# Prompt attention: the weights' division by their row sums moved from separate passes into the products that transpose them

## The chip, the cores and the metric

The kernel runs on one core of a Trainium2 chip. The metric is the device time of one execution in microseconds (us), lower is better. Engines are named as in the profile: PE is the TensorE matmul pipe (PEld its weight loads), DVE is VectorE, ACT is ScalarE, POOL is GpSimd, SP issues the DMAs.

## The reference, cut to what matters

One layer of a decoder for 1024 prompt tokens and 64 sample tokens, with a model width of 2048: a normalised and modulated input `h`, one input projection, three mixers side by side (dilated attention with 12 heads of 64, a spatial-gating MLP, an mLSTM), one output projection, a gate and the residual. The change lies in the attention of the prompt:

```
s = q k^T + bias                (per head, masked to the pattern; 1024 x 1024, causal)
p = exp(s - max(s)) / sum(exp(s - max(s)))      (over the keys)
o = p v
y_a = o * silu(z_a)
```

All inputs and outputs are float32. The reference forms three dilated patterns and combines them by their softmax denominators; the kernel does it in one softmax, with the logarithm of how many patterns hold a key added to the bias table.

## The kernel before, in words

Everything is kept with features on the partitions and the 1088 tokens on the free axis. The kernel goes through the input projection column by column (L252 to L254 are its three products: each weight tile and each input is split into a high and a low part of type float32r, and high times high, high times low and low times high are added up), and weaves the mixers' work between the columns. The prompt's attention is left for the last stage, where it is woven into the output projection.

**The last stage.** `project` runs twice over 16 output tiles. The first run takes the ten blocks of 128 features that the other two mixers have made (in pieces of 4, 2 and 4 blocks), the second the six blocks of the attention. For each piece and each of the three stretches of tokens (512, 320 and 256) it issues its products (`products`, L252 to L254) and then calls `tick()` once per block. Every call adds 0.345 to a counter, and each time this passes 1 the attention's generator does one step. So each engine's order of instructions is fixed when the program is written: some nine products of the projection, then one step of the attention, and so on. What is left of the attention after the first run is drained, and the second run follows.

**One step of the attention** (`attention`) may issue the value products of a block pair (`values`), the scores of a block of 128 queries (`scores`), the transposition of one block pair (`turn`), and what is due on ACT and DVE (`due`, sorted by the second number of `at`).

- `scores(e, m)` handles two blocks of queries, r = 0 and r = 1, with `nk = 128 * (2m + r + 1)` keys. Two products (L1445, L1446) put 512 columns of scores into PSUM, one DVE instruction (L1448) adds the bias, writes them to the tile `P` in SBUF and finds the rows' maxima. One step later ACT takes the exponential in place and sums the rows (`expo`, L1457). Two steps later `norm` takes the reciprocal of the sums (L1460, DVE) and multiplies the whole row of weights by it in place: for r = 1 on DVE (L1462), for r = 0 on ACT (L1464). The `P` tile is 256(m + 1) wide, so that for r = 0 its last 128 columns are not used.
- `turn(e, m, P, po, j)` makes up to four transposes (L1487) of 128 queries by 128 keys into the PSUM tile `pt`, three where the block pair lies on the diagonal. ACT copies `pt` to the high part `pH` (L1488), DVE subtracts to make the low part `pL` (L1489).
- `values` multiplies the value rows with `pH` (L1496) and `pL` (L1498) and adds up in PSUM; after the last pair the result is gated (L1502 to L1507) and stored.

`prep` fetches the next head's keys, queries, values and bias table; there POOL makes the low parts (L1406, L1411, L1417). POOL also makes the low parts of the weights (L99).

**Rows from other stages.** Four more lines serve the prediction for their durations. In the mLSTM, `first` issues a plain product of 128 by 128 (L938) and two transposes of the same size (L939, L940), one after the other, and L1003 is a product whose stationary operand has 32 columns. In the gating MLP L1148 is a plain product of 128 by 128, in fours. All of them have operands of type float32, without the high and low parts of the projection.

Of the kernel before, what the change touches and what calls it, by code (L numbers as in the profile page):

```python
# [11 lines left out]
FT = mybir.dt.float32  # L12
FR = mybir.dt.float32r
I32 = mybir.dt.int32
AF = mybir.ActivationFunctionType
OP = mybir.AluOpType
# [6 lines left out]
NSM = NB * NT  # L23
# [88 lines left out]
def body(tc, I, O):  # L112
    nc = tc.nc
    V, S, T, G, SP = nc.vector, nc.scalar, nc.tensor, nc.gpsimd, nc.sync
# [3 lines left out]
    def pool(name, st=None, **kw):  # L118
        return (st or stack).enter_context(tc.tile_pool(name=name, **kw))

    cp = pool("consts", bufs=1)
# [5 lines left out]
    bgs = ExitStack()  # L127
# [5 lines left out]
    def et(name="e"):  # L133
        return ev.tile([128, 388], FT, tag="e", name=name, bufs=7)
# [71 lines left out]
    def C(name, a=None, b=None, rows=128, r0=0):  # L206
        o, w = FO[name]
        a = 0 if a is None else a
        b = w if b is None else b
        return cst[r0:r0 + rows, o + a:o + b]  # L210

    ident = C("ident")
# [42 lines left out]

    ND9 = 9
    gate = cp.tile([128, KT, ND9], FT, name="gate")
    knew = cp.tile([128, 2, 2, NSM], FT, name="knew")
    qg8 = cp.tile([128, 1], FT, name="qg8")
    V.tensor_scalar(qg8, C("qg"), 0.125, None, op0=OP.mult)  # L260

# [276 lines left out]
    for k in range(2):  # L538
        for c, (t0, n) in enumerate(CH):
            for j in range(NST):  # L540
                ps = mm.tile([128, 512], FT, tag="mm", name="mm")
                wh, wl = w0[j // 2]
                o = 256 * (j % 2) + 128 * k
# [206 lines left out]
    st0.close()  # L750


    sel = pool("qk", bgs, bufs=1).tile([96, 3, 128], FR, name="sel")
    t = et("sel")
    SP.dma_start(t[:96, :128], I["sel"][:96])
    V.memset(sel.bitcast(FT), 0.0)
    for c in range(3):
        r = slice(32 * c, 32 * c + 32)
# [457 lines left out]
    def sample(qd):  # L1216
# [18 lines left out]
        for hf in range(2):  # L1235
# [49 lines left out]

            os_ = bank("os")
            pts = [turn(0)]
            yield
            pts.append(turn(1))
            yield  # L1290
            for i in range(5):
                v = kv_get()
                for x in range(2):
                    for b in range(4):
                        T.matmul(os_[32 * b:32 * b + 32, :256], pts[i][:, 128 * x + 32 * b:128 * x + 32 * b + 32],  # L1295
                                 v[:, b, 256 * x:256 * x + 256], start=(i == 0 and x == 0), stop=False,
                                 skip_group_check=True)
                if i < 4:
                    pts.append(turn(i + 2))
                yield  # L1300
# [82 lines left out]
    tp = pool("att", st4, bufs=1)  # L1383
# [43 lines left out]
    def at(d, order, f):  # L1427
        due.append((clk[0] + d, order, f))


    def scores(e, m):

        P = []
        for r in range(2):
            qb = 2 * m + r
            nk = 128 * (qb + 1)
            a = slice(128 * qb, 128 * qb + 128)
            s = tp.tile([128, 256 * (m + 1)], FT, tag=f"P{m}", name="P", bufs=2)
            mx = tp.tile([128, 6], FT, tag="mx", name="mx", bufs=6)
            np_ = 0  # L1440
            for k0 in range(0, nk, 512):
                w = min(512, nk - k0)
                wide = max(w, 256)
                ps = aps.tile([128, 512], FT, tag="a", name="s", bufs=5)
                T.matmul(ps[:, :wide], e["qs"][:, a], e["kd"][:, k0:k0 + wide], start=True, stop=False)  # L1445
                T.matmul(ps[:, :wide], e["qs"][:, a], e["kl"][:, k0:k0 + wide], start=False, stop=True)  # L1446
                x = k0 + 896 - 128 * qb
                V.tensor_tensor_reduce(s[:, k0:k0 + w], ps[:, :w], e["bt"][:, x:x + w], 1.0,  # L1448
                                       mx[:, np_ - 1:np_] if np_ else -3.0e38, op0=OP.add, op1=OP.max,
                                       accum_out=mx[:, np_:np_ + 1])  # L1450
                np_ += 1
                if k0 + 512 < nk:
                    yield
            V.tensor_scalar(mx[:, 2:3], mx[:, np_ - 1:np_], -1.0, None, op0=OP.mult)

            def expo(s=s, mx=mx, nk=nk):
                S.activation(s[:, :nk], s[:, :nk], AF.Exp, bias=mx[:, 2:3], accum_out=mx[:, 3:4])  # L1457

            def norm(s=s, mx=mx, nk=nk, r=r):
                V.reciprocal(mx[:, 4:5], mx[:, 3:4])  # L1460
                if r:
                    V.tensor_scalar(s[:, :nk], s[:, :nk], mx[:, 4:5], None, op0=OP.mult)  # L1462
                else:
                    S.activation(s[:, :nk], s[:, :nk], AF.Copy, scale=mx[:, 4:5])  # L1464

            at(1, 0, expo)
            at(2, 1, norm)
            P.append(s)
            if r or m:
                yield  # L1470
        return P

    def turn(e, m, P, po, j):

        pt = aps.tile([128, 512], FT, tag="a", name="pt", bufs=5)
        pH = tp.tile([128, 512], FR, tag="pH", name="pH", bufs=3)
        pL = tp.tile([128, 512], FR, tag="pL", name="pL", bufs=3)
        f = 128 if j == m else 0
        if f:
            V.memset(pH[:, 0:128].bitcast(FT), 0.0)  # L1480
            V.memset(pL[:, 0:128].bitcast(FT), 0.0)
        for b in range(2):
            for r in range(2):
                k = 128 * (2 * j + b)
                o = 256 * (1 - b) + 128 * r
                if o >= f:
                    T.transpose(pt[:, o:o + 128], P[r][:, k:k + 128], ident)  # L1487
        S.copy(pH[:, f:], pt[:, f:])  # L1488
        at(0, 3, lambda: V.tensor_tensor(pL[:, f:], pt[:, f:], pH[:, f:].bitcast(FT), op=OP.subtract))  # L1489
        return pH, pL  # L1490
# [21 lines left out]
    def all_scores(e):  # L1512
        for hd in range(HA):
            pg = prep(hd + 1) if hd + 1 < HA else loads(KB[:3])
            nxt = None
            for m in range(4):
                g = scores(e, m)
                while True:
                    try:
                        next(g)  # L1520
                    except StopIteration as x:
                        P = x.value
                        break
                    yield
                    if pg is not None and m and clk[0] % 2:
                        try:
                            next(pg)
                        except StopIteration as x:
                            nxt, pg = x.value, None
                po = []  # L1530
                for j in range(m + 1):
                    tq.append((clk[0] + 2, (e, m, P, po, j)))
            while pg is not None:
                try:
                    next(pg)
                except StopIteration as x:
                    nxt, pg = x.value, None
            e = nxt
# [250 lines left out]
```

## Time and profile before

| what | before |
|---|---|
| median of 3 runs | 2487.4 us (2485.78 to 2488.67) |
| profiled execution, its time | 2489.15 us |
| its span | 2487.2 us |
| PE busy | 2435.5 us, 98% of the span |
| DVE busy | 939.0 us, 38% |
| ACT busy | 746.2 us, 30% |
| POOL busy | 646.5 us, 26% |

The span runs from the first to the last instruction of the profiled execution; the other 1.95 us of its time lie around it. In the rows of groups, the two numbers after the first bar are the busy time in us and the mean of one instruction in ns, and behind the second bar stand the idle time of the engine ahead of them in us and what ended it. A matmul's own duration counts from its start to its modelled end, and the next one starts before that end; how many ns a matmul takes of a dense stream is read from the chain of work, whose pieces do not overlap.

### The profile page before, as it was taken

The page shows a single profiled execution, that of the slowest core. Times are in us where ns is not written, and L with a number is a line of the kernel's source. Part 1 is how long each engine was busy: PE and PEld are TensorE (multiplying, and loading weights), DVE is VectorE, ACT ScalarE, POOL GpSimd, SP SyncE. Part 2 cuts the span into 40 slices and gives each one's busy share as a digit, 9 for nine tenths or more (in the row PEclk, how much of TensorE's full clock was granted, in tenths as well). Part 3 has the DMA queues.
Part 4 walks back from the last instruction along what each step waited for, and adds up shares of the span by engine and source line. Part 5 has one row for each costly group of instructions (what it writes and reads, how often), then busy time and mean ns, then how long its engine had stood idle before and what let it go on. Part 6 is the DMA issues. An engine that isn't in the chain of part 4 may idle for free.

```text
span 2487.2 us, 39837 instructions
## 1 busy us (share of the span) xinstructions
PE 2435.5 (98%) x15879; PEld 2228.4 (90%) x15879; DVE 939.0 (38%) x2489; ACT 746.2 (30%) x1638; POOL 646.5 (26%) x502
## 2 busy tenths in 40 slices
PE   5999999999999999999999999999999999999999
PEld 2678799999999999999999999898889899888898
DVE  4673100323232322313342002433212688887322
ACT  3222211323223232323321112222113566666210
POOL 2541122231312222322222222111212333332321
PEclk8999999999999999999999999999999999999999
DMA  8864621111211111121313415746565655554454
GB/s 280 287 231 146 223 68 39 57 65 53 63 55 57 62 60 53 48 74 49 118 58 101 153 48 213 255 164 236 207 222 193 198 158 155 150 151 134 159 170 143
DMA packets 157081, 332.95 MB, mean 134 GB/s; under 512 B 21770, under 2 KB 76834, under 8 KB 149216
## 3 DMA queue, kind: packets, MB, share of 16 engines
q1 hardware_dynamic: 156896, 330.41, 40.8%
q8 instruction: 125, 2.05, 0.4%
q14 instruction: 60, 0.49, 0.1%
HBM read 284.26 MB, written 54.55 MB: 136 GB/s over the span
## 4 chain that ended last, share of the span: by engine, by line
PE 91%; DVE 3%; DMA 3%; issue 1%; ACT 1%; SPq 1%; POOL 0%; DVEq 0%; ACTq 0%; POOLq 0%
PE mm L252 26%; PE mm L254 25%; PE mm L253 25%; PE ad L342 2%; PE pt L1487 2%; PE os L1295 1%; PE sq L1245 1%; PE o L1498 1%; PE s L1446 1%; PE o L1496 1%; PE s L1445 1%; DMA x<-in_xT 1%; DMA ad<-in_adaw 1%; PE b L938 0%; PE b L970 0%
## 5 line engine op out<-in xcount | busy, mean ns | idle before, releaser
L252 PE MATMUL mm<-hH,wh 128*128 128x384 f32 (+1 forms) x3168 | 1063.2, 336 | 10.0 <-ACT hH L425 8.4
L253 PE MATMUL mm<-hL,wh 128*128 128x384 f32 (+1 forms) x3168 | 1034.4, 327 | 2.6 <-DVE hL L431 2.6
L254 PE MATMUL mm<-hH,wl 128*128 128x384 f32 (+1 forms) x3168 | 1035.8, 327 | 0.0
L99 POOL TENSOR_TENSOR wl<-wraw,wh 128x512 fp32r<-128x512 f32 x344 | 445.7, 1303 | 1570.2 <-ACT wh L98 1466.8
L252 PEld LDWEIGHTS mm<-hH,wh 128*128 128x128 f32 x3168 | 595.5, 188 | 75.3 <-issue 40.0
L253 PEld LDWEIGHTS mm<-hL,wh 128*128 128x128 f32 x3168 | 595.9, 188 | 4.7 <-DVE hL L431 3.6
L254 PEld LDWEIGHTS mm<-hH,wl 128*128 128x128 f32 x3168 | 594.9, 188 | 0.0
L98 ACT CAST wh<-wraw 128x512 fp32r<-128x512 f32 x344 | 200.9, 596 | 379.9 <-PE mm L253 269.6
L252 PE MATMUL mm<-yH,wh 128*128 128x512 f32 (+2 forms) x768 | 262.3, 341 | 2.8 <-DVE xo L1583 2.8
L254 PE MATMUL mm<-yH,wl 128*128 128x512 f32 (+2 forms) x768 | 252.3, 329 | 1.1 <-POOL wl L99 1.1
L253 PE MATMUL mm<-yL,wh 128*128 128x512 f32 (+2 forms) x768 | 252.4, 329 | 0.0
L254 PEld LDWEIGHTS mm<-yH,wl 128*128 128x128 f32 x768 | 145.3, 189 | 12.5 <-POOL wl L99 1.5
L252 PEld LDWEIGHTS mm<-yH,wh 128*128 128x128 f32 x768 | 145.4, 189 | 12.2 <-issue 3.0
L253 PEld LDWEIGHTS mm<-yL,wh 128*128 128x128 f32 x768 | 145.6, 190 | 8.9
L894 DVE SCALAR_TENSOR_TENSOR u<-R,cw,u 128x384 f32<-128x384 f32 (+1 forms) x108 | 62.0, 574 | 213.4 <-ACT u L892 210.8
L1583 DVE SCALAR_TENSOR_TENSOR xo<-mm,gate,xo 128x512 f32<-128x512 f32 (+2 forms) x96 | 54.3, 568 | 116.1 <-PE mm L254 107.8
L1488 ACT CAST pH<-pt 128x512 fp32r<-128x512 f32 (+1 forms) x120 | 65.2, 543 | 81.1 <-PE pt L1487 80.4
L1489 DVE TENSOR_TENSOR pL<-pt,pH 128x512 fp32r<-128x512 f32 (+1 forms) x120 | 74.1, 618 | 15.6 <-ACT pH L1488 15.5
L1457 ACT ACTIVATE P<-P,mx 128x128 f32<-128x128 f32 (+3 forms) x96 | 74.5, 777 | 4.2 <-issue 2.9
L1487 PE MATMUL pt<-cst,P 128*128 128x128 f32 x432 | 68.9, 274 | 6.3 <-DVE P L1462 5.9
L1487 PEld LDWEIGHTS pt<-cst,P 128*128 128x128 f32 x432 | 52.7, 140 | 19.3 <-DVE P L1462 9.2
L1448 DVE CUSTOM_DVE_ANT_0 P<-s,btab 128x512 f32<-128x512 f32 (+2 forms) x96 | 56.1, 584 | 34.2 <-PE s L1446 33.9
(324 smaller groups left out, 2409.7 us busy)
## 6 DMA issues: line engine op xcount, KB each, us to landing
wraw<-in_win SPq DMA_DIRECT2D x264, 256.0 KB
ad<-in_adaw SPq DMA_DIRECT2D x96, 512.0 KB
kv<-in_ck SPq DMA_DIRECT2D x30, 1024.0 KB
kv<-in_cv SPq DMA_DIRECT2D x30, 1024.0 KB
wraw<-in_wout SPq DMA_DIRECT2D x48, 256.0 KB
x<-in_xT SPq DMA_DIRECT2D x16, 544.0 KB
yraw<-yD SPq DMA_DIRECT2D x16, 544.0 KB
xo<-in_xT SPq DMA_DIRECT2D x16, 544.0 KB
```

The lines of the kernel that those rows point to most:

```text
L98: self.nc.scalar.copy(wh[:, :n], raw[:, :n])
L99: self.nc.gpsimd.tensor_tensor(wl[:, :n], raw[:, :n], wh[:, :n].bitcast(FT), op=OP.subtract)
L252: T.matmul(ps[:, :n], wh[:, a], rh[:, t0:t0 + n], start=first and i == 0, stop=False)
L253: T.matmul(ps[:, :n], wh[:, a], rl[:, t0:t0 + n], start=False, stop=False)
L254: T.matmul(ps[:, :n], wl[:, a], rh[:, t0:t0 + n], start=False, stop=last and i == len(rows) - 1)
L894: V.scalar_tensor_tensor(u[:, :npr], R[:, j:j + npr], cw[:, m, j:j + 1], u[:, :npr], op0=OP.mult, op1=OP.add)
L1448: V.tensor_tensor_reduce(s[:, k0:k0 + w], ps[:, :w], e["bt"][:, x:x + w], 1.0, mx[:, np_ - 1:np_] if np_ else -3.0e38, op0=OP.add, op1=OP.max,
L1457: S.activation(s[:, :nk], s[:, :nk], AF.Exp, bias=mx[:, 2:3], accum_out=mx[:, 3:4])
L1487: T.transpose(pt[:, o:o + 128], P[r][:, k:k + 128], ident)
L1488: S.copy(pH[:, f:], pt[:, f:])
L1489: at(0, 3, lambda: V.tensor_tensor(pL[:, f:], pt[:, f:], pH[:, f:].bitcast(FT), op=OP.subtract))
L1583: V.scalar_tensor_tensor(x[:, t0:t0 + npr], ps[:, :npr], gate[:, dm, 0:1], x[:, t0:t0 + npr], op0=OP.mult, op1=OP.add)
```

## The change

The weights stay as ACT's exponential left them. For each block of queries `norm` now makes a diagonal matrix of 128 by 128, the identity times the reciprocal sums (one DVE instruction, L1463 of the changed kernel). For r = 0 it goes to the free columns of `P`, for r = 1 to a tile of its own, `dg`, with three buffers. The passes of L1462 and L1464 are gone. In `turn`, where a transpose stood (the data as the stationary operand, the identity as the moving one), a product stands now: the data as the stationary operand, the diagonal matrix as the moving one. So out of `pt` come the transposed weights, already divided. The tile `knew`, used in an earlier stage alone, moves to a pool that is closed before the last stage.

```
-    knew = cp.tile([128, 2, 2, NSM], FT, name="knew")
...
-    sel = pool("qk", bgs, bufs=1).tile([96, 3, 128], FR, name="sel")
+    qkp = pool("qk", bgs, bufs=1)
+    sel = qkp.tile([96, 3, 128], FR, name="sel")
+    knew = qkp.tile([128, 2, 2, NSM], FT, name="knew")
...
             mx = tp.tile([128, 6], FT, tag="mx", name="mx", bufs=6)
+            dg = tp.tile([128, 128], FT, tag="dg", name="dg", bufs=3) if r else s[:, nk:nk + 128]
...
-            def norm(s=s, mx=mx, nk=nk, r=r):
+            def norm(mx=mx, dg=dg):
                 V.reciprocal(mx[:, 4:5], mx[:, 3:4])
-                if r:
-                    V.tensor_scalar(s[:, :nk], s[:, :nk], mx[:, 4:5], None, op0=OP.mult)
-                else:
-                    S.activation(s[:, :nk], s[:, :nk], AF.Copy, scale=mx[:, 4:5])
+                V.tensor_scalar(dg, ident, mx[:, 4:5], None, op0=OP.mult)
...
-            P.append(s)
+            P.append((s, dg))
...
                 if o >= f:
-                    T.transpose(pt[:, o:o + 128], P[r][:, k:k + 128], ident)
+                    T.matmul(pt[:, o:o + 128], P[r][0][:, k:k + 128], P[r][1], start=True, stop=True)
```

On PE, in the middle of the second head's scores, the order before has the four transposes of a pair (`pt<-cst,P`) between the next scores and the projection:

```order
L1446 MATMUL s<-kl,qs 128x512
L1487 MATMUL pt<-cst,P 128x128 x4
L252 MATMUL mm<-yH,wh 128x256
L253 MATMUL mm<-yL,wh 128x256
L254 MATMUL mm<-yH,wl 128x256
```

In the changed kernel the same place reads as follows. `pt<-P` is a product whose diagonal matrix lies in `P` itself (r = 0), `pt<-dg,P` one with the tile `dg` (r = 1); the scores' lines have moved by two.

```order
L1448 MATMUL s<-kl,qs 128x512
L1487 MATMUL pt<-P 128x128
L1487 MATMUL pt<-dg,P 128x128
L1487 MATMUL pt<-P 128x128
L1487 MATMUL pt<-dg,P 128x128
L252 MATMUL mm<-yH,wh 128x256
```

Four instructions stand in the place of four, and nothing else of PE's order has moved; over the program 432 transposes became 432 products.

On DVE, at the place where the third pair of query blocks of a head is normalised (m = 2, r = 1), before:

```order
L1481 MEMSET pL 128x128
L1460 RECIPROCAL mx<-mx 128x1
L1462 TENSOR_SCALAR P<-P,mx 128x768
L1505 TENSOR_TENSOR t<-o,t 64x256
L1507 SCALAR_TENSOR_TENSOR t<-t,zt 64x256
```

And with the change:

```order
L1481 MEMSET pL 128x128
L1462 RECIPROCAL mx<-mx 128x1
L1463 TENSOR_SCALAR dg<-cst,mx 128x128
L1505 TENSOR_TENSOR t<-o,t 64x256
L1507 SCALAR_TENSOR_TENSOR t<-t,zt 64x256
```

The pass over 768 columns has become one over 128 in the same place; where r = 0, one over 128 is new on DVE right behind the reciprocal, and ACT's pass is gone without anything in its place. The orders of POOL and of SP are the same in both kernels, and so is every engine's order ahead of the attention's first `norm`.

## The prediction

> **What bounds the kernel now.** I read the busy times of the page first, then the chain that ended last, then the stretch of the last stage in which the attention runs, 1945 to 2320 us after the span's start.
>
> ```profile
> span 2487.2 us, 39837 instructions
> PE 2435.5 (98%) x15879; PEld 2228.4 (90%) x15879; DVE 939.0 (38%) x2489; ACT 746.2 (30%) x1638; POOL 646.5 (26%) x502
> ```
>
> ```profile
> PE 91%; DVE 3%; DMA 3%; issue 1%; ACT 1%; SPq 1%; POOL 0%; DVEq 0%; ACTq 0%; POOLq 0%
> ```
>
> ```profile
> core 0: us, PE busy (x) PEld busy (x) DVE busy (x) ACT busy (x) POOL busy (x), PEclk, DMA share, GB/s
> 1945.00:2320.00 375.00, 365.61 (x2428) 332.35 (x2428) 296.95 (x908) 236.36 (x487) 125.54 (x80) 1.00 0.53 150
> ```
>
> PE is busy for 98% of the whole span, 91% of the chain is PE, and the stretch that the change touches is no different: 365.6 of its 375.0 us, at the full granted clock (1.00). DVE (297.0 us, 79%) and ACT (236.4 us, 63%) have room there. So a change in this stretch is worth what it does to PE's own stream, plus what it does to the 9.4 us in which PE stands. The waits of PE in that stretch say whom it stands for:
>
> ```profile
> engine line waited for: us in total, times, longest us
> PE pt L1487 <- DVE P L1462: 5.9, 6, 1.5
> PE o L1498 <- DVE pL L1489: 1.8, 4, 1.1
> PE o L1496 <- ACT pH L1488: 1.2, 1, 1.2
> PE pt L1487 <- DVE mx L1448: 0.3, 1, 0.3
> ```
>
> They make 9.2 us. The largest is the pass that the change removes from DVE, and the transposes of L1487 are what waits for it; but it is 5.9 us in 6 events, of 120 groups of transposes.
>
> **What it removes: two sets of passes.** The groups of that stretch, L1462 with its four widths apart:
>
> ```profile
> L1462 DVE TENSOR_SCALAR P<-P,mx 128x256 f32<-128x256 f32 x12 | 4.2, 354 | 0.4
> L1462 DVE TENSOR_SCALAR P<-P,mx 128x512 f32<-128x512 f32 x12 | 11.2, 931 | 0.4
> L1462 DVE TENSOR_SCALAR P<-P,mx 128x768 f32<-128x768 f32 x12 | 12.7, 1060 | 0.5
> L1462 DVE TENSOR_SCALAR P<-P,mx 128x1024 f32<-128x1024 f32 x12 | 10.7, 894 | 0.4
> ...
> L1464 ACT ACTIVATE P<-P,mx 128x128 f32<-128x128 f32 (+3 forms) x48 | 34.5, 720 | 12.1 <-DVE mx L1460 12.0
> ...
> L1480 DVE MEMSET pH<- 128x128 f32 x48 | 7.9, 165 | 0.0
> ```
>
> DVE loses 4.2 + 11.2 + 12.7 + 10.7 = 38.8 us, ACT 34.5 us. Neither engine is the bound, so none of these 73 us comes off the time by itself. They count only through PE's 9.2 us of waits.
>
> **What it adds on DVE: 96 diagonal matrices of 128x128.** The trace has no such instruction. From below it is bounded by the store of the same size without an input, 165 ns (L1480), from above by the same operation on twice the columns, 354 ns (L1462, 128x256). I take 290 ns, nearer to the latter since it is the same operation with half the columns: 96 x 0.29 = 28 us. For r = 0 this is new work on DVE, for r = 1 a shorter pass. DVE's sum falls by about 11 us, ACT's by 34.5 us, and this hides beside PE, as the passes did. If that cover were gone, 28 us is the most that it could cost.
>
> **What it adds on PE: 432 products for 432 transposes.** This is the term that decides. What a transpose takes of PE's stream is shown by two pieces of the chain, a group of four and one of three where PE waits for nothing:
>
> ```profile
> 1970.48 0.44 PE pt L1487 x4
> ```
>
> ```profile
> 1973.67 0.33 PE pt L1487 x3
> ```
>
> That is 110 ns each, and by 432 it is 47.5 us of the stretch. A plain product of the same size and type does not stand at this place before, but elsewhere in the same program there are some. First, how many records one makes: L938 is a plain product and L939 a transpose, issued by the same loop side by side, so that both stand equally often in the program.
>
> ```profile
> L938 PE MATMUL b<-qT,kT 128*128 128x128 f32 x96 | 18.5, 274 | 0.0
> L939 PE MATMUL b<-cst,kT 128*128 128x128 f32 x48 | 13.1, 273 | 0.0
> ```
>
> The product leaves 96 records where the transpose leaves 48: on this chip a float32 product is carried out as two matmuls, each with its weight load, and the transpose as one. Then what they take of the stream, again from the chain:
>
> ```profile
> 764.06 0.22 PE b L938 x2
> 764.28 0.11 PE b L939
> ```
>
> ```profile
> 1260.89 0.89 PE mx L1148 x8
> ```
>
> One product (L938, two records) takes 0.22 us, and the transpose right behind it 0.11 us. Four products of L1148 in a row, with the same shapes as the change's four, are eight records and 0.89 us, or 222.5 ns for one. So each exchange costs 222.5 - 110 = 112.5 ns, and 432 of them 432 x 0.1125 = 48.6 us. Nothing hides it: PE's stream is dense in the whole stretch, and the projection's products stand right behind.
>
> On this the Trainium skill, "TensorE: Matmul & The Clock Gate", section Terms, has a rule that speaks against the change even more: it says that the transpose mode is 4 times faster for FP32. By that rule the exchange would cost three transposes' time, and the sum would be 142.6 us in place of 48.6. The rows above show a factor of two at this size, and the measurement decides; the rule is kept as a rival below.
>
> **What becomes of PE's waits.** The transposes wait for exponential, reciprocal and pass; now for exponential, reciprocal and a diagonal matrix. At m = 2 the pass at its shortest takes twice what I put for the matrix, so that some tenths of a us of each of the 6 waits go. But much of such a wait isn't the length of the pass. The stretch around 2101 us, in order of time:
>
> ```profile
> 2101.16 2.40 POOL L1406 TENSOR_TENSOR kl<-kr,kd 128x1024 fp32r<-128x1024 f32 x1 [3.21 <-ACT kd L1405]
> 2101.26 2.58 DVE L1462 TENSOR_SCALAR P<-P,mx 128x512 f32<-128x512 f32 x1
> ```
>
> The pass over 512 columns started 0.10 us behind a POOL instruction of 2.40 us and took 2.58 us, though the pass over 1024 columns takes 0.89 us on the mean. DVE's pass stood until POOL was through. The diagonal matrix is the same operation on the same engine, with both operands in SBUF, and will stand likewise; now for r = 0 as well, where ACT did it without such a wait. The Trainium skill, "SBUF — State Buffer", section Who interferes with whom, names tensor_scalar among the operations that can take a port pair shared with GpSimd, the later one being blocked fully; the two rows agree. So one gain (shorter passes, 34.5 us less on ACT, 11 us less on DVE, also for `pH` and `pL`) stands against one loss (96 exposed instructions instead of 48). The ends: all 9.2 us of waits go, or they double. I take a third gone, -3.1 us, since the load on both engines falls and the stretch grows by an eighth.
>
> Where a wait goes, next is the projection's product behind it, which needs weights that POOL makes two pieces ahead. The wait for the buffers of `dg` (three, each freed by the last product of its pair of query blocks) falls behind no work: a buffer comes round again with the third pair after it, and is written seven steps or more behind the pair's last scores, while the pair's products are issued two to five steps behind them. `knew` is written in an earlier stage in the same place of DVE's order, and its move costs nothing.
>
> **The sum.** 48.6 - 3.1 = +45.5 us. Against the profiled execution (2489.15 us, of which 2487.2 is the span) that is 2534.7 us; this execution lies 1.75 us above the median of the runs, 2487.4 us, and a median is what is measured, so I forecast 2487.4 + 45.5 = 2533 us (rounded).
>
> **Rivals.**
>
> *The diagonal matrices stand behind POOL and PE stands behind them.* The shortest passes of the three wider forms, in the order of time:
>
> ```profile
> 1977.03 0.75 DVE L1462 TENSOR_SCALAR P<-P,mx 128x1024 f32<-128x1024 f32 x1
> ```
>
> ```profile
> 1983.46 0.49 DVE L1462 TENSOR_SCALAR P<-P,mx 128x512 f32<-128x512 f32 x1
> ```
>
> ```profile
> 2026.45 0.62 DVE L1462 TENSOR_SCALAR P<-P,mx 128x768 f32<-128x768 f32 x1
> ```
>
> Twelve of each, with 0.35 us for 256 columns, are 26.5 us; the 48 passes took 38.8 us, so 12.3 us were standing. 96 exposed instructions would stand 24.6 us; if all of it reaches PE beside the old waits, the time is 2487.4 + 48.6 + 24.6 = 2560.6 us. For it: PE did wait for L1462. Against: of 12.3 us that stood, PE felt at most 5.9, and the matrices of r = 0 are made a step ahead of those of r = 1 wherever m is above 0. Chance 0.06.
>
> *Four transposes' time for a product.* 432 x 3 x 0.110 = 142.6, less 3.1: 2626.9 us. The rows of L938 and L1148 speak against it, and nothing in the trace for it. Chance 0.02.
>
> *Not slower: the second matmul of a product costs next to nothing here.* The point from which this decides: with all 9.2 us of waits gone, a product may take 110 + 9200/432 = 131 ns for no loss. One row shows matmuls from float32 operands that follow each other so fast, those of L1003, whose stationary operand has 32 columns:
>
> ```profile
> 771.70 1.01 PE b L1003 x16
> ```
>
> It is 63 ns a record, 126 ns a product; 432 x 0.016 - 9.2 = -2.3, or 2485 us. Against: the change's stationary operand has 128 columns, as L1148's, and all rows of that shape show 0.11 us a record. Chance 0.03.
>
> *The change doesn't do what it says:* the product with a diagonal matrix is carried out as one matmul like a transpose. Then only waits go, 3.1 to 9.2 us, around 2481 us. L938 and L1148 speak against it. Chance 0.02.
>
> **How the numbers follow.** The forecast has 0.87. Its own bounds are the waits' ends, 2487.4 + 48.6 - 9.2 = 2526.8 and 2487.4 + 48.6 + 9.2 = 2545.2, with the runs' spread of about 1.5 us at either end: 2525 to 2547. These leave out 0.13 for the rivals, so the range need not reach to them. A measurement of this kernel can tell about 0.2%, 5 us, from no change. Faster by more than that comes from parts of the last two rivals, 0.03; within it, 0.02; slower, 0.95.
>
> **What would show it.** Right: L1487 with 864 records, groups of eight at 0.89 us in the chain, the stretch of the attention about 45 us longer with PE still at 97% or more, all other stages as before; DVE with 96 instructions of 0.2 to 0.35 us in the place of L1462, some of over 1 us when POOL is at work. Wrong: 432 records, or eight of them well under 0.8 us; PE waits for the diagonal matrices of 20 us and more; or a stage ahead of the attention that has moved.

## The result, and the profile after

| what | before | after |
|---|---|---|
| median of 4 runs | 2486.9 us (2485.78 to 2488.67) | 2529.76 us (2527.79 to 2535.3) |
| ratio to before | | 1.0172, 95% interval 1.0159 to 1.0184 |
| profiled execution, its span | 2487.2 us | 2525.7 us |

The kernel became slower by 42.9 us between the medians; 45.5 were forecast. The busy times of the page after, and the group of products with the tile `dg`, with its counterpart for r = 0:

```profile
span 2525.7 us, 40801 instructions
PE 2482.0 (98%) x16311; PEld 2283.3 (90%) x16311; DVE 957.8 (38%) x2537; ACT 715.5 (28%) x1590; POOL 644.7 (26%) x502
...
L1487 PE MATMUL pt<-dg,P 128*128 128x128 f32 x480 | 85.5, 276 | 2.6 <-DVE dg L1463 2.6
...
L1487 PE MATMUL pt<-P 128*128 128x128 f32 x384 | 73.9, 274 | 0.2 <-DVE mx L1450 0.2
```

PE has 16311 - 15879 = 432 records more, and L1487 has 480 + 384 = 864, where it had 432. In order of time on PE, a group of four of them in the second head (the chain of after covers the last stretch alone, so the stream is read from the starts):

```profile
1969.27 0.38 PE L1487 MATMUL pt<-P 128*128 128x128 f32 x2
1969.49 0.39 PE L1487 MATMUL pt<-dg,P 128*128 128x128 f32 x2
1969.71 0.39 PE L1487 MATMUL pt<-P 128*128 128x128 f32 x2
1969.93 0.39 PE L1487 MATMUL pt<-dg,P 128*128 128x128 f32 x2
```

Each product has two records, and the next one starts 0.22 us later. Where the attention's stretch begins and ends is read from its first score product and its last subtraction, in the rows of the tiles `s` and `pL`. Before:

```profile
L1445 PE MATMUL s<-kd,qs x144: 274/364/398, 1947.7 to 2297.0; 128*128 128x512 f32 x72, 128*128 128x256 f32 x48, 128*128 128x384 f32 x24
```

```profile
L1489 DVE TENSOR_TENSOR pL<-pt,pH x120: 486/674/692, 1954.5 to 2314.8; 128x512 fp32r<-128x512 f32 x72, 128x384 fp32r<-128x384 f32 x48
```

And after:

```profile
L1447 PE MATMUL s<-kd,qs x144: 277/389/415, 1944.0 to 2334.5; 128*128 128x512 f32 x72, 128*128 128x256 f32 x48, 128*128 128x384 f32 x24
```

```profile
L1489 DVE TENSOR_TENSOR pL<-pt,pH x120: 485/675/693, 1951.8 to 2354.1; 128x512 fp32r<-128x512 f32 x72, 128x384 fp32r<-128x384 f32 x48
```

From 1947.7 to 2314.8 are 367.1 us, from 1944.0 to 2354.1 are 410.1 us: +43.0 us, the whole of the change. That the stretch begins 3.7 us earlier in the one profiled execution after is mostly from the first 400 us, where the inputs arrive (PE was busy for 369.65 us there and for 366.97 before); the change has nothing in that stage, and the runs of one kernel differ by as much.

PE's waits in the stretch after, and its busy time:

```profile
engine line waited for: us in total, times, longest us
PE pt L1487 <- DVE dg L1463: 2.6, 5, 1.0
PE o L1498 <- DVE pL L1489: 1.6, 3, 0.9
PE pt L1487 <- DVE mx L1450: 0.2, 1, 0.2
```

```profile
1944.00:2357.00 413.00, 408.46 (x2840) 382.60 (x2839) 314.05 (x954) 203.88 (x435) 119.96 (x77) 1.00 0.48 136
```

The waits fell from 9.2 to 4.4 us. The diagonal matrices on DVE, for r = 0 and r = 1:

```profile
L1463 DVE TENSOR_SCALAR P<-cst,mx 128x128 f32<-128x128 f32 x48 | 26.9, 561 | 1.7
...
L1463 DVE TENSOR_SCALAR dg<-cst,mx 128x128 f32<-128x128 f32 x48 | 25.7, 536 | 1.7
```

They took 52.6 us. The row of the tile `P` has the least, the median and the most of those for r = 0, in ns:

```profile
L1463 DVE TENSOR_SCALAR P<-cst,mx x48: 285/286/2585, 1949.8 to 2336.2; 128x128 f32<-128x128 f32 x48
```

In DVE's and POOL's order of time, 71 of the 96 took 0.29 us or less. Each of the other 25 began while a POOL instruction was running and ended 0.07 to 0.09 us after the end of one; together these 25 took 25.2 us more than 25 of the shortest. This is one of them, for r = 1, where POOL's instruction began 0.15 us earlier:

```profile
2183.85 2.39 POOL L1407 TENSOR_TENSOR kl<-kr,kd 128x1024 fp32r<-128x1024 f32 x1 [8.44 <-ACT kd L1406]
2184.00 2.32 DVE L1463 TENSOR_SCALAR dg<-cst,mx 128x128 f32<-128x128 f32 x1
```

So DVE, which lost 38.8 us of passes, had 52.6 us of matrices in their place, and the standing of the matrices is a standing behind POOL.

### The profile page after: what moved, and what is told of

It reads as the page before. It is cut to its first block, busy times and chain, and to the rows that moved or that the text cites. A ratio compares the mean times of both kernels' runs of the same rounds, so it can differ in the third digit from the quotient of the medians.

```text
span 2525.7 us, 40801 instructions
## 1 busy us (share of the span) xinstructions
PE 2482.0 (98%) x16311; PEld 2283.3 (90%) x16311; DVE 957.8 (38%) x2537; ACT 715.5 (28%) x1590; POOL 644.7 (26%) x502
## 5 line engine op out<-in xcount | busy, mean ns | idle before, releaser
L1487 PE MATMUL pt<-dg,P 128*128 128x128 f32 x480 | 85.5, 276 | 2.6 <-DVE dg L1463 2.6
L1489 DVE TENSOR_TENSOR pL<-pt,pH 128x512 fp32r<-128x512 f32 (+1 forms) x120 | 75.5, 629 | 21.5 <-ACT pH L1488 19.7
L1487 PE MATMUL pt<-P 128*128 128x128 f32 x384 | 73.9, 274 | 0.2 <-DVE mx L1450 0.2
L1487 PEld LDWEIGHTS pt<-dg,P 128*128 128x128 f32 x480 | 69.0, 192 | 3.5 <-issue 2.3
```

The costliest lines, as they stand in the source:

```text
L1487: T.matmul(pt[:, o:o + 128], P[r][0][:, k:k + 128], P[r][1], start=True, stop=True)
```

## The experiments

Theory A is the prediction's: the time is 432 more matmuls on a dense PE, less some of PE's waits. Theory B has it in the matrices on DVE that stand behind POOL. Theory C, against A's reading of the rows, says that a plain product costs twice a transpose whatever its operands' type. Ratios are to the kernel before, run beside each experiment on the same chip; its medians in the three sets were 2490.71, 2488.13 and 2488.25 us.

**Transposes with the matrices kept**

```
-                    T.matmul(pt[:, o:o + 128], P[r][0][:, k:k + 128], P[r][1], start=True, stop=True)
+                    T.transpose(pt[:, o:o + 128], P[r][0][:, k:k + 128], P[r][1])
...
-                V.tensor_scalar(dg, ident, mx[:, 4:5], None, op0=OP.mult)
+                V.tensor_scalar(dg, ident, 1.0, None, op0=OP.mult)
```

> The changed kernel with its products turned back into transposes; the 96 matrices are still made on DVE in the same places, by the identity times 1.0, and are the transposes' moving operand, so that every wait for DVE stays. It leaves the normalisation of the weights out. Theory A (the time is the second matmul of each product, 112.5 ns by 432 on a dense PE): 432 records of L1487, and 2530 - 48.6 = 2481 us, within 3. Theory B (the time is the 96 matrices on DVE, standing behind POOL, and PE standing behind them): it stays within 10 us of 2530.

Measured: 2489.45 us, a ratio of 1.000 (0.999 to 1.0009), 432 records. B falls: with every matrix still made on DVE (43.1 us in all; times a constant, the shortest takes 198 ns and not 285), the whole slowdown is gone. But A's 2481 us was missed as well. The time is that of the kernel before, and so are PE's waits:

```profile
engine line waited for: us in total, times, longest us
PE pt L1487 <- DVE dg L1463: 4.4, 6, 1.2
PE o L1498 <- DVE pL L1489: 2.6, 5, 1.2
PE o L1496 <- ACT pH L1488: 1.2, 1, 1.2
PE pt L1487 <- DVE mx L1450: 0.2, 1, 0.2
```

They make 8.4 us, against 9.2 before. Passes off and matrices on are, together, worth nothing that the runs tell apart.

**Products by the identity, passes kept**

```
-                    T.transpose(pt[:, o:o + 128], P[r][:, k:k + 128], ident)
+                    T.matmul(pt[:, o:o + 128], P[r][:, k:k + 128], ident, start=True, stop=True)
```

> The kernel before, its passes of normalisation kept, with plain products by the identity in the place of the transposes; the result is the same. Theory A: 864 records of L1487, and 2487 + 48.6 = 2535.6 us, down to 2531 if the longer stretch swallows a part of the 9.2 us of waits. Theory B: within 4 us of 2487, since DVE has no matrices to make.

Measured: 2533.1 us, a ratio of 1.0174 (1.0156 to 1.0191), level with the change itself. By the ratio that is +43.3 us; on the 2487 us of the expectation it would be 2530 us, 1 us under the lower end that A had named and within the interval. The chain of this kernel shows a group of four at the very place:

```profile
1975.11 0.89 PE pt L1487 x8
```

Eight records in 0.89 us, as L1148 had foretold. And the waits, with passes and engines' work as before:

```profile
engine line waited for: us in total, times, longest us
PE pt L1487 <- DVE P L1462: 3.6, 4, 1.4
PE o L1498 <- DVE pL L1489: 0.8, 3, 0.4
PE o L1496 <- ACT pH L1488: 0.3, 1, 0.3
```

4.7 us, where the kernel before has 9.2. Nothing was taken off DVE or ACT here. Only PE's own stream was made longer, so its lengthening is what lowered the waits. The likely reason is that more of PE's time lies between two steps of the attention, and the other engines come in time more often; that was not tested by itself.

**No passes, no matrices**

```
             def norm(s=s, mx=mx, nk=nk, r=r):
-                V.reciprocal(mx[:, 4:5], mx[:, 3:4])
...
+                pass
```

> The kernel before without the reciprocals and without both sets of passes, so the weights are not normalised; the transposes stay. It prices the removal by itself. Theory A: only PE's waits can go, 9.2 us at most, so 2478 to 2484 us. If the passes on ACT and DVE were worth more than PE's visible waits, as a rival to my reading of the stage has it, under 2475 us. If they are hidden wholly: 2487 us.

Measured: 2482.36 us, a ratio of 0.9966 (0.9954 to 0.9978), or -8.5 us. PE stands for 3.3 us of the stretch:

```profile
1950.00:2313.00 363.00, 359.67 (x2413) 330.11 (x2413) 261.47 (x762) 203.49 (x436) 120.73 (x78) 1.00 0.54 154
```

This lies in A's range: the 73 us of passes are worth little more than what PE waited for them (by the interval, 5.5 to 11.5 us). Beside the first experiment it says that the matrices on DVE cost that gain again.

**Operands of float32r**

```
-            s = tp.tile([128, 256 * (m + 1)], FT, tag=f"P{m}", name="P", bufs=2)
+            s = tp.tile([128, 256 * (m + 1)], FR, tag=f"P{m}", name="P", bufs=2)
...
-            dg = tp.tile([128, 128], FT, tag="dg", name="dg", bufs=3) if r else s[:, nk:nk + 128]
+            dg = tp.tile([128, 128], FR, tag="dg", name="dg", bufs=3) if r else s[:, nk:nk + 128]
...
```

> The changed kernel with the weights and the matrices kept as float32r, so that the product with the diagonal matrix takes float32r operands; it leaves out the low bits of scores and weights. Theory A (a float32 product costs two matmuls, one of float32r costs one): 432 records, 0.44 us for four in the stream, 2480 to 2485 us. Theory C (a plain product costs twice a transpose whatever its type): 2525 us or more.

Measured: 2492.77 us, a ratio of 1.001 (1.000 to 1.0019).

```profile
L1487 PE MATMUL pt<-dg,P 128*128 128x128 f32 x240 | 54.9, 277 | 5.1 <-DVE dg L1463 5.1
L1487 PE MATMUL pt<-P 128*128 128x128 f32 x192 | 43.5, 243 | 0.2 <-DVE mx L1450 0.2
```

A group of four in the chain of this kernel:

```profile
1969.48 0.39 PE pt L1487 x4
```

One record for each product, 432 in all, four of them in 0.39 us, and no slowdown: C falls. The cost of the change isn't that of a plain product, it is the second matmul that a float32 product makes. The 2480 to 2485 us that A named were missed, as in the first experiment: the matrices on DVE are still there, and PE's waits in the stretch make 10.5 us, 5.1 of them for `dg`.

**The matrices on ACT**

```
-                V.tensor_scalar(dg, ident, mx[:, 4:5], None, op0=OP.mult)
+                S.activation(dg, ident, AF.Copy, scale=mx[:, 4:5])
```

> The changed kernel with its 96 diagonal matrices made on ACT instead of DVE; the result is the same. Theory A now has two parts: 48.6 us of added matmuls, and PE's idle time, which the DVE matrices that stand behind POOL (561 and 536 ns on the mean against 285 at the least) keep up. If the second part is right, the matrices on ACT all take one duration within 10%, PE waits for none of them over 0.5 us, and the time is 2 to 6 us under the changed kernel's, a ratio of 1.015 to 1.0165. If where they are made does not matter, the ratio is 1.017 to 1.018.

Measured: 2524.88 us, a ratio of 1.0147 (1.0133 to 1.016), against 1.0172 of the change (in another set of runs, with intervals that touch: 1.0159 is its lower end). The matrices now take between 386 and 407 ns, the row for `dg`:

```profile
L1463 ACT ACTIVATE dg<-cst,mx x48: 386/402/405, 1952.8 to 2342.1; 128x128 f32<-128x128 f32 x48
```

```profile
engine line waited for: us in total, times, longest us
PE pt L1487 <- ACT dg L1463: 0.6, 2, 0.4
PE o L1498 <- DVE pL L1489: 0.6, 2, 0.4
```

None of them stood, and PE waits for 1.2 us in all. The time is a little lower than was expected (1.0147, where 1.015 to 1.0165 was named). The stretch from the first score product to the last subtraction is 404.8 us long, where the change has 410.1. On ACT a matrix takes longer than DVE's shortest, and ACT is still the better place.

**Transposes, with matrices on ACT**

```
-                    T.matmul(pt[:, o:o + 128], P[r][0][:, k:k + 128], P[r][1], start=True, stop=True)
+                    T.transpose(pt[:, o:o + 128], P[r][0][:, k:k + 128], P[r][1])
...
-                V.tensor_scalar(dg, ident, mx[:, 4:5], None, op0=OP.mult)
+                S.activation(dg, ident, AF.Copy, scale=1.0)
```

> Transposes as in the kernel before, no passes, and 96 matrices of identity times 1.0 made on ACT instead of on DVE, as the transposes' moving operand; it leaves the normalisation of the weights out. The same kernel with the matrices on DVE was level with the kernel before (1.000), and without passes and matrices the ratio was 0.9966. If the DVE matrices' standing behind POOL took the difference, this gets nearly all of it: 0.996 to 0.998. If any 96 instructions between the exponential and the transposes take it, 0.999 to 1.001.

Measured: 2477.85 us, a ratio of 0.996 (0.9946 to 0.9973). The 96 matrices cost nothing measurable on ACT and some 8.5 us on DVE (1.000 against 0.9966). The reciprocals are kept in this kernel, and the kernel without normalisation lacks them, so it is not they that cost those 8.5 us. A reservation: with a constant factor the matrices are shorter than in the change (294 ns at the least on ACT for 386, 198 on DVE for 285), and ACT doesn't wait for DVE's reciprocal. The experiment before, with the true factors, points the same way.

**Products alone, no passes and no matrices**

```
-                V.reciprocal(mx[:, 4:5], mx[:, 3:4])
...
+                pass
...
-                    T.transpose(pt[:, o:o + 128], P[r][:, k:k + 128], ident)
+                    T.matmul(pt[:, o:o + 128], P[r][:, k:k + 128], ident, start=True, stop=True)
```

> The kernel before without reciprocals and passes, with plain products by the identity in the place of the transposes; it leaves the normalisation out. It prices the matmuls where PE hardly waits for anything: 48.6 us on top of the 0.9966 of the kernel without normalisation, or 2487 x 0.9966 + 48.6 = 2527 us, a ratio of 1.0162, less up to 3 us of idle time that was left there, so 1.015 to 1.0165. If half of the products' time were hidden there, it is 1.007.

Measured: 2525.69 us, a ratio of 1.0147 (1.0134 to 1.0161). Over the kernel without normalisation that is 0.0181 of 2488.25 us, 45.0 us, with 3.3 us of PE's idle time to be swallowed there, of which 0.9 us is left:

```profile
1950.00:2355.00 405.00, 404.15 (x2829) 379.79 (x2828) 265.65 (x756) 202.45 (x431) 119.13 (x76) 1.00 0.48 137
```

So no large part of the matmuls is hidden: 45.0 + 2.4 = 47.4 us of the 48.6, with an interval of some 4 us on the difference of two ratios. The ratio itself lies just under the expected 1.015.

**Half of the change**

```
-            def norm(mx=mx, dg=dg):
+            def norm(s=s, mx=mx, dg=dg, nk=nk, r=r):
...
-                V.tensor_scalar(dg, ident, mx[:, 4:5], None, op0=OP.mult)
+                if r:
+                    V.tensor_scalar(dg, ident, mx[:, 4:5], None, op0=OP.mult)
+                else:
+                    S.activation(s[:, :nk], s[:, :nk], AF.Copy, scale=mx[:, 4:5])
...
-                    T.matmul(pt[:, o:o + 128], P[r][0][:, k:k + 128], P[r][1], start=True, stop=True)
+                    if r:
+                        T.matmul(pt[:, o:o + 128], P[r][0][:, k:k + 128], P[r][1], start=True, stop=True)
+                    else:
+                        T.transpose(pt[:, o:o + 128], P[r][0][:, k:k + 128], ident)
```

> The changed kernel with the products and matrices for r = 1 alone; r = 0 keeps ACT's pass and its transposes; the result is the same. 240 products of the 432, so theory A has 240 x 0.1125 = 27.0 us of matmuls less 2 to 5 us of idle time: a ratio of 1.009 to 1.010. Theory B (matrices behind POOL) has half of the 43 us of the change, 1.0085, at 48 matrices, and cannot be told from A by the time; it is told by the records, 672 of L1487, and by PE's waits for DVE, which would be 10 us or more.

Measured: 2509.41 us, a ratio of 1.0086 (1.0068 to 1.0103), with 480 + 192 = 672 records, and 3.0 us of waits of PE for DVE's matrices. The expected 1.009 lies within the interval, as does B's 1.0085; the time can't tell them apart, but B's 10 us of waits aren't there.

**Both sets of passes on ACT, without the change**

```
-                if r:
-                    V.tensor_scalar(s[:, :nk], s[:, :nk], mx[:, 4:5], None, op0=OP.mult)
-                else:
-                    S.activation(s[:, :nk], s[:, :nk], AF.Copy, scale=mx[:, 4:5])
+                S.activation(s[:, :nk], s[:, :nk], AF.Copy, scale=mx[:, 4:5])
```

> The kernel before with both sets of passes on ACT, the transposes kept; the result is the same. Leaving both passes out was worth a ratio of 0.9966. If PE's waits come from DVE's passes standing behind POOL, this gets a part of that: 0.997 to 0.9985, though ACT gets some 40 us more of work. If ACT becomes what PE waits for, it is 1.000 or more.

Measured: 2484.45 us, a ratio of 0.9987 (0.9978 to 0.9996), -3.2 us: the one kernel with the full computation that beats both, by less than the 0.2% that I called distinguishable, though its interval excludes 1. The gain is a little smaller than the 0.997 to 0.9985 that were expected. PE now waits for ACT's passes:

```profile
engine line waited for: us in total, times, longest us
PE pt L1484 <- ACT P L1461: 4.6, 7, 1.3
PE o L1493 <- ACT pH L1485: 1.6, 1, 1.6
PE o L1495 <- DVE pL L1486: 1.6, 3, 1.1
```

**The passes exchanged between the engines**

```
-                if r:
+                if not r:
                     V.tensor_scalar(s[:, :nk], s[:, :nk], mx[:, 4:5], None, op0=OP.mult)
```

> The kernel before with the passes of r = 0 on DVE and those of r = 1, which PE waits for last, on ACT; the result is the same. Same work on each engine, within 5 us. If the waits come from the last pass standing behind POOL, the ratio is 0.997 to 0.999; if only the load on the engines counts, 1.000.

Measured: 2488.87 us, a ratio of 1.0006 (0.9997 to 1.0015). The idea that the last pass's standing is what counts falls, and the 1.000 of the other one lies within the interval: with ACT making the last pass, PE waits 6.5 us for ACT.

## Why the prediction was right, point by point

*The exchange of 432 transposes for products, +48.6 us.* Right in mechanism and size. Two records for each product, 0.89 us for eight of them in the stream, at the very place; 240 of the 432 products gave half of the slowdown (which by the time alone would fit theory B as well); one record for each (float32r) gave none; products without anything else gave 45 us on a PE that had little idle time to lose.

*The rule of four transposes' time.* Four products took 0.89 us and four transposes 0.44, a factor of two, as L938 and L1148 said. The Trainium skill, "TensorE: Matmul & The Clock Gate", section Terms, calls the transpose mode 4 times faster for FP32. The measured factor for float32 products of 128 by 128 in a dense stream is two, and it decides.

*The matrices on DVE, 28 us beside other work and up to 24.6 us of standing.* The shortest took 285 ns for the 290 estimated, and all of them together 52.6 us for 28 + 24.6. The standing was priced right and came in full, but I used it only for a rival, and in the forecast DVE's sum was to fall by 11 us where it rose by 13.8. That the rival failed nonetheless, PE not waiting for more, is shown by PE's waits: 2.6 us for `dg`, 4.4 us in all.

*PE's waits, a third of 9.2 us gone.* The term that was mis-sized, and one of its two reasons was wrong. The prediction gave two: less load on ACT and DVE, and a stretch that grows by an eighth. The first failed: passes off and matrices on leave the time as it was (1.000), since what the removal gains (-8.5 us) the standing matrices take again. What did shorten PE's waits is the second, the lengthening of PE's own stream: products alone, with all passes kept, took them from 9.2 to 4.7 us, and gave +43.3 us by the ratio for +48.6 of matmuls. The change measures +42.9, which is 48.6 less 5.7, where I took off 3.1. So the sign came out right by one reason of the two, and that the size came within 3 us is partly luck. Of the 5.7, 4.8 us are the waits that the profile names (9.2 less 4.4); the rest, 0.9 us, is under what the runs tell apart.

*The rival by which the kernel gets no slower.* It needed products of 131 ns or less. In the changed kernel each product starts 0.22 us after the one before, so this rival never came near.

Where the gain of the removal went is shown further by two stretches, each from the first score product to the last subtraction, both with transposes and without passes. The first is the kernel with the matrices on DVE, the second the one without matrices:

```profile
1951.80:2318.90 367.10, 358.37 (x2390) 327.36 (x2389) 295.07 (x953) 202.96 (x435) 118.77 (x76) 1.00 0.54 153
```

```profile
1950.20:2309.50 359.30, 355.96 (x2390) 326.75 (x2389) 260.92 (x761) 202.90 (x435) 119.25 (x77) 1.00 0.55 156
```

With the matrices the stretch is 7.8 us longer, which agrees with the 8.5 us between the ratios. PE's idle time in it is 8.7 us against 3.3, so 5.4 of the 7.8 us are waits, and not for the matrices alone (4.4 us in the first kernel): PE waits for the work behind them too, such as the subtractions of L1489. The other 2.4 us lie in PE's busy time, since the same 2390 matmuls are busy for longer. What stays open is why. Matmuls that follow each other less closely behind a wait would explain it, but no run separates this.

## What to carry to other kernels

To fold a scaling into a transposition by a diagonal matrix, ask first how many matmuls the product becomes with the operands' type: here, with float32, it was two for the transpose's one, and since TensorE was the bound, each cost nearly its full time. Work taken off engines that have room is worth about the waits of the bound engine that it ends: here 73 us of passes had some 8.5 us in them. And a short DVE instruction can cost as much as a long one if it has to stand behind GpSimd; ACT may be the better place though its own duration is longer.

## What the runs showed of the hardware that was not expected

On ACT the making of one diagonal matrix took 386 to 407 ns without one exception, on DVE 285 to 2585 ns, and each of the 25 long ones on DVE began while POOL was at work and ended just behind one of its instructions. With the matrices' values constant, 96 of them cost some 8.5 us on DVE and nothing measurable on ACT. And a stream of PE that is made longer by 48.6 us swallowed 4.5 us of PE's own waits, with no other engine's work changed.
